# Decode attention finished beside the last gate pairs, and w_pc's stage fed one to two tiles ahead

## The chip, the cores and the metric

The kernel runs on one core of one Trainium2 chip. The metric is the device time of one execution in microseconds (us). The kernel before took 1598.49 us (median of three runs, 1595.0 to 1600.42). A difference within 0.3% (about 5 us) counts here as no change.

Engines are named as in the profile: PE (TensorE matmul), PEld (its weight loads), DVE (VectorE), ACT (ScalarE), POOL (GpSimd), SP (SyncE). SP and POOL issue nearly all DMAs, each in its own order.

## The reference, cut to what matters

```
h = RMSNorm_pre(x)
[q,k,v,ga | cb,cc,ch,gc | ma,mc] = h @ w_in
a = StickBreakingAttn(q,k,v) * silu(ga)       # 8 heads of 128; prompt: 528 tokens, causal
c = cb * conv3_causal(cc * ch) * silu(gc)
m = sigmoid(ma + b) * (a @ w_pa) + sigmoid(mc + b) * (c @ w_pc)
x = x + RMSNorm_post(m @ w_out)
# attention: A[t,s] = sigmoid(z_ts) * prod_{s<j<t} (1 - sigmoid(z_tj)), in log space
# decode: 8 sequences of 4 new tokens, each with 512 cached keys and values in 4 pages of 128
```

Prompt (512 tokens and 16 meta tokens) and decode (32 tokens) go through the same projections together: 560 columns, D_MODEL = 2048. All arithmetic is fp32: operands of the large products are split into a high and a low part and three matmuls are made of each product. Every weight block therefore passes through ACT (`whi`, L240) and DVE (`wlo`, L241) before TensorE may use it.

## The kernel before, in words

Order of the stages: norm and first queries; heads 0 to 3 attended at once (`head_now`); keys and values of heads 4 to 7 projected and put away in DRAM (`head_later`: `k_scr`, `vn_scr`, `qt_scr`); 36 gate pairs; the stage of `w_pc`; the stage of `w_pa`; the output projection.

**Gate pairs.** Each pair makes two 128-column blocks of `h @ w_in` with seven products of 24 matmuls (`seven`, L944). After each pair `dec_group()` (L875) is called, which takes some steps of the decode attention out of the generator `decode_steps()`. Steps 1 to 24 of it belong to the head stages. Then, in order: 40 steps of logits, each one page of keys (`kpage`) against four queries, 16 dot products on DVE (L754); the softmax in two steps and the exponentials in a third (L476, L800 to L815); eight steps of value products: each loads eight pages of values (`vpage`, L730, 9 buffers, issued by POOL) and multiplies them on TensorE (L829: 16 matmuls of four column groups, and in every second step 8 more with the new tokens' values), and every second step copies the sum out (`ob`, L849), transposes it (L852) and multiplies it into `sg_s` (L857). Softmax activations are pinned behind what stands before them on ACT, the value matmuls behind what stands before them on TensorE.

The counter `n` in `dec_group` sets at which pair the steps are emitted. Before: two per pair for n = 2 to 4, one for n = 5 to 20, then 2 and 1 in turn up to n = 32; softmax and exponentials at n = 34 to 36; then the first eight value pages are loaded; the value products come in the next stage.

The order on each engine is not the program's order. A scheduler of the library makes it when the kernel is built: among the instructions that its timing model holds ready it takes the first in program order, and a tile waits for a free buffer of its pool. [...]

**The stage of w_pc** (L1113 to L1155) makes 16 tiles `c @ w_pc` (48 matmuls each, L256, moving operand `c_hl`), multiplies each by its gate `gt` (loaded from `gate_scr`, L1150; L1153) and stores it again (L1154). Between the tiles heads 4 to 7 are attended (`HERE`: head 4 before tile 0, then before tiles 3, 6 and 9): scores (L608), softplus on ACT (L467 to L470) and DVE (L473 to L476), mask (L622), suffix products (L677), exponential (L681), output (L687). `gated` (L1124) multiplies an output by its gate rows and splits it into `a_hl` for the next stage. It is also called for heads 0 to 3, whose outputs lie in `a_scr`. In the kernel before

- the loads of `gt` (L1150), of the gate rows `sg` (L1129) and of `a_scr` (L1146) stand just ahead of their use, and share four buffers (pool `g3`, tag `gt`);
- the splits of a head's keys, values and queries (`khi`, `vhi`, `qhi`, L494 and L495) go into single buffers, just ahead of its scores;
- `dec_step(1)` before each tile takes one step of the value products.

Of the kernel before, what the change touches and what calls it, by code (L numbers as in the profile page):

```python
# [9 lines left out]
F32 = mybir.dt.float32  # L10
# [7 lines left out]
P = 128  # L18
D = 2048
KD = D // P  # L20
# [5 lines left out]
T = TP + TS  # L26
# [6 lines left out]
TQ = T - NMETA  # L33
HQ = TQ // 2
HU = HQ + 2
PQ = SEQ
# [6 lines left out]
H = 8  # L43
# [8 lines left out]
NOW = 4  # L52
# [8 lines left out]
def hybrid_step_kernel(  # L61
# [6 lines left out]
    nc = tc.nc  # L68
# [19 lines left out]
    def mm_ps():  # L88
        return ps.tile([P, 512], F32, tag="mm", name="mm", bufs=3)
# [4 lines left out]
    def o_ps():  # L94
        return ps.tile([P, 512], F32, tag="o", name="o", bufs=1)
# [148 lines left out]
    def weights(srcs):  # L244

        return [w_split(w_load(s)) for s in srcs]
# [210 lines left out]
    sg_scr = dram.tile([H, P, TQ], F32, name="sg_scr")  # L457
    a_scr = dram.tile([NOW, P, PQ], F32, name="a_scr")
# [4 lines left out]
    gate_scr = dram.tile([KD, P, 2, TQ], F32, name="gate_scr")  # L463
# [20 lines left out]
    d3ctx, hlctx, hctx, nctx = (ExitStack() for _ in range(4))  # L484
    hl = []
# [6 lines left out]
    def split_evac(hi, lo, raw_hi, raw_lo, scale=None):  # L492
        if scale is None:
            act.copy(hi, raw_hi)  # L494
# [53 lines left out]
    def k_split(pl, kr):  # L548
        khi = pl.tile([P, T], F32R, name="khi")
        klo = pl.tile([P, T], F32R, name="klo")  # L550
        split_evac(khi, klo, kr, kr)
        return khi, klo

    def v_split(pl, vn):
        vhi = pl.tile([P, 5, P], F32R, name="vhi", bufs=1)
        vlo = pl.tile([P, 5, P], F32R, name="vlo", bufs=1)
        split_evac(vhi[:, 0:4, :], vlo[:, 0:4, :], vn[:, 0:4, :], vn[:, 0:4, :])
        split_evac(vhi[0:16, 4, :], vlo[0:16, 4, :], vn[0:16, 4, :], vn[0:16, 4, :])
        return vhi, vlo
# [30 lines left out]
            return None  # L590
        return v_split(pl, vn)

    def attend(pl, h, khi, klo, vhi, vlo, qr, pl_a=None, after=None):

        qhi = pl.tile([P, T], F32R, name="qhi")
        qlo = pl.tile([P, T], F32R, name="qlo")
        split_evac(qhi[:, NMETA:TP], qlo[:, NMETA:TP], qr, qr)

        b = bsb[:, h:h + 1]
        gt = {}  # L600
# [33 lines left out]
        for g in GROUPS:  # L634
# [29 lines left out]
        ot = o_ps()  # L664
# [26 lines left out]
    def head_now(h):  # L691

        qr = hp.tile([P, TQ], F32, name="qr", bufs=2)[:, 0:PQ]
        nc.sync.dma_start(qr, qt_scr[h][:, 0:PQ])
        khi, klo = k_split(np_, k_proj(h))
        dec_step(1 if h else 0, "part")
        vhi, vlo = v_proj(h, np_)
        dec_step(1, "part")
        q_proj(NOW + h)
        dec_step(2, "part")  # L700
        ot = attend(np_, h, khi, klo, vhi, vlo, qr)
# [8 lines left out]
        v_proj(h)  # L710
        dec_step(2, "part")

    def head_loads(h):
        kr = hl[0].tile([P, T], F32, name="kr")
        nc.sync.dma_start(kr, k_scr[h])
        qr = hl[0].tile([P, PQ], F32, name="qr")
        nc.sync.dma_start(qr, qt_scr[h][:, 0:PQ])
        vn = hl[0].tile([P, 5, P], F32, name="vn")
# [154 lines left out]
    def dec_group():  # L873

        n = n_group[0] = n_group[0] + 1  # L875
        if n <= 32:
            dec_step((0, 2, 2, 2)[n - 1] if n <= 4 else 1 if n <= 20 else 1 + n % 2, "logits")
        else:
            dec_step(1)

    np_ = nctx.enter_context(tc.tile_pool(name="now", bufs=2))
    tc.keep_in_program_order(act.preload_act_table_set(LNEXP))
# [124 lines left out]
    def by_query(m, half):  # L1007
        return slice(half * HQ, (half + 1) * HQ)
# [61 lines left out]
    def q_tile(name):  # L1070
        return gp.tile([P, 2, HU], F32, tag="cv", name=name, bufs=3).rearrange("p a b -> p (a b)")[:, 0:TQ]
# [15 lines left out]
    for j in range(0, KD, 2):  # L1087
        for w, c in ((0, COL_MA), (1, COL_MC)):
            gs = [q_tile("g") for _ in range(2)]
            for m, half, b in pair(c + j * P, HQ):  # L1090
                act.activation(gs[m][:, by_query(m, half)], b, AF.Sigmoid, bias=gate_bias(j + m, w))
            if j + 2 * w == KD:
                tc.keep_in_program_order(act.preload_act_table_set(LNEXP))
            for m in range(2):
                gate_out(j + m, w, gs[m])
            dec_group()
            if j + w == 14:

                after = hl[0].tile([P, P], F32, name="after")
                dve.tensor_scalar_add(after, neg_u.bitcast(F32), 1.0)  # L1100
                loaded = head_loads(NOW)
    dec_step(64, "values")
    assert "values" in dec_at and "end" not in dec_at
    gctx.close()
    tctx.close()

# [1 line left out]
    QH = ((0, HQ), (HQ, TQ))  # L1108
    g3ctx, cctx, mctx = (ExitStack() for _ in range(3))
    g3 = g3ctx.enter_context(tc.tile_pool(name="g3", bufs=4))  # L1110
    c_hl = tok.tile([P, KD, TQ], F32R, tag="A", name="c_hl")
    a_hl = tok.tile([P, KD, TQ], F32R, tag="B", name="a_hl")
    cp = cctx.enter_context(tc.tile_pool(name="later", bufs=1))  # L1113
    cp2 = cctx.enter_context(tc.tile_pool(name="later2", bufs=1))

    for k in range(0, 8, 2):
        cr = g3.tile([P, 2, TQ], F32, tag="gt", name="cr")
# [4 lines left out]
    def gated(h, x, sg):  # L1122

        dve.tensor_mul(sg, x, sg)  # L1124
        split_evac(a_hl[:, h, 0:PQ], a_hl[:, 8 + h, 0:PQ], sg, sg)

    def sg_load(h):
        sg = g3.tile([P, 2, TQ], F32, tag="gt", name="sg")
        nc.sync.dma_start(sg[:, 0, 0:PQ], sg_scr[h][:, 0:PQ])  # L1129
        return sg  # L1130

    def head_here(h):
        kr, vn, qr = loaded if h == NOW else head_loads(h)
        ot = attend(cp, h, *k_split(cp, kr), *v_split(cp, vn), qr, cp2, after)
        gated(h, ot, sg_load(h)[:, 0, 0:PQ])


    HERE = {0: 4, 3: 5, 6: 6, 9: 7}
    for j in range(KD):
        if j in HERE:  # L1140
            head_here(HERE[j])
        dec_step(1)
        if j in HERE:
            k = j // 3
            x = sg_load(k)
            nc.sync.dma_start(x[:, 1, 0:PQ], a_scr[k])  # L1146
            gated(k, x[:, 1, 0:PQ], x[:, 0, 0:PQ])
        cs = slice(j * P, (j + 1) * P)
        gt = g3.tile([P, 2, TQ], F32, tag="gt", name="gt")[:, 1, :]
        nc.sync.dma_start(gt, gate_scr[j][:, 1, :])  # L1150
        oc = gemm(weights([w_pc[0][:, cs]]), lambda k: (c_hl[:, k, :], c_hl[:, 8 + k, :]), QH)
        for ob, s in qparts(oc):
            dve.tensor_mul(gt[:, s], ob, gt[:, s])  # L1153
        pool.dma_start(gate_scr[j][:, 1, :], gt)  # L1154
    dec_step(64)  # L1155
    split_evac(a_hl[:, 0:8, PQ:TQ], a_hl[:, 8:16, PQ:TQ], sg_s, sg_s)
    d3ctx.close()
    hlctx.close()
    dctx.close()
    cctx.close()  # L1160
# [7 lines left out]
    for k in range(8):  # L1168
        ms = []
        for j in (k, k + 8):  # L1170
            gt = g3.tile([P, 2, TQ], F32, tag="gt", name="gt")
# [7 lines left out]
        y, x = (ms[0][:, 1, slice(*s)] for s in QH)  # L1179
# [31 lines left out]
    with tc.tile_pool(name="outp", bufs=1) as op:  # L1211
# [107 lines left out]
        j = KD - 2  # L1319
# [117 lines left out]
```

## Time and profile before

| | us |
|---|---|
| median of three runs | 1598.49 |
| the profiled execution | 1598.94 |
| its span in the profile | 1597.3 |
| gate pairs, from 369 to 1139 of the span | 770 |
| stage of w_pc, from 1139.4 to 1307.8 | 168.4 |
| stage of w_pa, to 1405 | 97 |

Times inside the span count from its start. "Busy" is the time in which at least one instruction of the engine ran; in brackets stands the number of instructions. A row of waits reads: who waited, for whom, us in total, times, the longest. PEclk is the granted share of TensorE's clock.

### The profile page before, as it was taken

The page shows a single profiled execution, that of the slowest core. Times are in us where ns is not written, and L with a number is a line of the kernel's source. Part 1 is how long each engine was busy: PE and PEld are TensorE (multiplying, and loading weights), DVE is VectorE, ACT ScalarE, POOL GpSimd, SP SyncE. Part 2 cuts the span into 40 slices and gives each one's busy share as a digit, 9 for nine tenths or more (in the row PEclk, how much of TensorE's full clock was granted, in tenths as well). Part 3 has the DMA queues.
Part 4 walks back from the last instruction along what each step waited for, and adds up shares of the span by engine and source line. Part 5 has one row for each costly group of instructions (what it writes and reads, how often), then busy time and mean ns, then how long its engine had stood idle before and what let it go on. Part 6 is the DMA issues. An engine that isn't in the chain of part 4 may idle for free.

```text
span 1597.3 us, 32319 instructions
## 1 busy us (share of the span) xinstructions
PE 1567.6 (98%) x12172; PEld 1533.7 (96%) x12172; DVE 1268.8 (79%) x3574; ACT 752.7 (47%) x1339; POOL 234.6 (15%) x428
## 2 busy tenths in 40 slices
PE   9999999999999999999999999999899999999997
PEld 8999999999999999999999999999897789999997
DVE  6328999956799999999999996667666657877776
ACT  6335555435444444444454444446645543355562
POOL 1033333222111011010011100001203320000000
PEclk9999999999999999999999999999999999999999
DMA  8246556344555445355356554433868875433345
GB/s 247 81 137 180 169 164 187 110 127 138 167 162 146 139 140 150 117 152 159 107 180 187 161 155 130 125 121 115 279 186 265 253 240 179 152 101 99 100 137 187
DMA packets 300674, 252.77 MB, mean 158 GB/s; under 512 B 11521, under 2 KB 268613, under 8 KB 299701
## 3 DMA queue, kind: packets, MB, share of 16 engines
q1 hardware_dynamic: 272021, 160.45, 34.7%
q0 software_dynamic: 28368, 89.98, 17.0%
q8 instruction: 95, 1.56, 0.4%
q14 instruction: 62, 0.51, 0.1%
q10 hardware_dynamic: 128, 0.27, 0.1%
HBM read 217.95 MB, written 32.71 MB: 157 GB/s over the span
## 4 chain that ended last, share of the span: by engine, by line
PE 89%; DMA 4%; issue 2%; DVE 2%; ACT 1%; POOL 0%; DVEq 0%; POOLq 0%; SPq 0%; ACTq 0%
PE mm L944 32%; PE mm L256 24%; PE o L944 23%; DMA vpage<-in_cache_v 2%; PE mm L321 2%; PE z L321 1%; PE z L677 1%; PE o L687 1%; DMA raw<-in_w_in 1%; PE z L608 1%; PE z L1378 1%; DMA sg<-a_scr 1%; DMA gt<-gate_scr 1%; DVE wlo L241 1%; PE tp L829 0%
## 5 line engine op out<-in xcount | busy, mean ns | idle before, releaser
L240 ACT CAST whi<-raw 128x1024 fp32r<-128x1024 f32 x247 | 259.4, 1051 | 356.0 <-PE mm L944 122.3
L241 DVE TENSOR_TENSOR wlo<-raw,whi 128x1024 fp32r<-128x1024 f32 x247 | 301.2, 1221 | 82.9 <-ACT whi L240 81.5
L944 PE MATMUL mm<-h_hi,whi 128*128 128x272 f32 (+1 forms) x1152 | 332.6, 289 | 0.0
L944 PE MATMUL mm<-h_lo,whi 128*128 128x272 f32 (+1 forms) x1152 | 332.4, 289 | 0.0
L944 PE MATMUL mm<-h_hi,wlo 128*128 128x272 f32 (+1 forms) x1152 | 332.3, 290 | 0.0
L944 PE MATMUL o<-t_hi,whi 128*128 128x272 f32 (+1 forms) x864 | 250.0, 289 | 1.0 <-DVE c L970 1.0
L944 PE MATMUL o<-t_lo,whi 128*128 128x272 f32 (+1 forms) x864 | 250.2, 290 | 0.0
L944 PE MATMUL o<-t_hi,wlo 128*128 128x272 f32 (+1 forms) x864 | 249.8, 289 | 0.0
L754 DVE CUSTOM_DVE_ANT_0 junk<-kpage,qb 128x128 f32<-128x128 f32 x1024 | 245.1, 285 | 3.7 <-DMA qb<-q_scr 3.3
L944 PEld LDWEIGHTS mm<-h_hi,whi 128*128 128x128 f32 x1152 | 217.4, 189 | 0.0
L944 PEld LDWEIGHTS mm<-h_hi,wlo 128*128 128x128 f32 x1152 | 216.9, 189 | 0.1
L944 PEld LDWEIGHTS mm<-h_lo,whi 128*128 128x128 f32 x1152 | 216.8, 188 | 0.1
L241 DVE TENSOR_TENSOR wlo<-s,whi 128x1024 fp32r<-128x1024 f32 x126 | 154.0, 1222 | 63.9 <-ACT whi L240 62.5
L240 ACT CAST whi<-s 128x1024 fp32r<-128x1024 f32 x126 | 132.0, 1048 | 152.9 <-PE mm L944 52.8
L256 PE MATMUL mm<-h_lo,whi 128*128 128x280 f32 (+1 forms) x640 | 187.7, 293 | 0.0
L256 PE MATMUL mm<-h_hi,wlo 128*128 128x280 f32 (+1 forms) x640 | 187.1, 293 | 0.0
L256 PE MATMUL mm<-h_hi,whi 128*128 128x280 f32 (+1 forms) x640 | 186.7, 292 | 0.0
L944 PEld LDWEIGHTS o<-t_hi,whi 128*128 128x128 f32 x864 | 162.9, 189 | 1.5 <-DVE c L970 1.5
L944 PEld LDWEIGHTS o<-t_lo,whi 128*128 128x128 f32 x864 | 163.4, 189 | 0.5 <-issue 0.4
L944 PEld LDWEIGHTS o<-t_hi,wlo 128*128 128x128 f32 x864 | 163.1, 189 | 0.1
L256 PEld LDWEIGHTS mm<-h_lo,whi 128*128 128x128 f32 x640 | 120.4, 188 | 0.8
L256 PEld LDWEIGHTS mm<-h_hi,whi 128*128 128x128 f32 x640 | 120.5, 188 | 0.5
(390 smaller groups left out, 3181.1 us busy)
## 6 DMA issues: line engine op xcount, KB each, us to landing
raw<-in_w_in SPq DMA_DIRECT2D x192, 512.0 KB, 4.3
kpage<-in_cache_k POOLq DMA_DIRECT2D x64, 256.0 KB, 3.5
qb<-q_scr POOLq DMA_DIRECT2D x32, 512.0 KB, 5.7
vpage<-in_cache_v POOLq DMA_DIRECT2D x64, 256.0 KB, 5.8
raw<-in_w_out SPq DMA_DIRECT2D x32, 512.0 KB, 4.1
gate_scr<-g POOLq DMA_DIRECT2D x32, 272.0 KB, 4.6
gt<-gate_scr POOLq DMA_DIRECT2D x16, 544.0 KB, 3.9
raw<-in_w_pc SPq DMA_DIRECT2D x16, 512.0 KB, 4.4
```

The costliest lines, as they stand in the source:

```text
L240: act.copy(hi, x)
L241: dve.tensor_sub(lo, x, hi.bitcast(F32))
L256: pe.matmul(o, lhsT=w, rhs=r[:, t0:t1], start=(k == 0 and n == 0), stop=(k == nk - 1 and n == 2))
L321: pin(pe.matmul(o, lhsT=l, rhs=r[:, k, t0:t1], start=(start and m == 0), stop=(stop and m == 2), skip_group_check=True))
L608: pe.matmul(zt[:m, c0:c0 + n], lhsT=l[:, s0:s0 + m], rhs=r[:, ts:ts + n], start=(c0 == 0 and i == 0), stop=(i == 2), skip_group_check=True)
L677: pe.matmul(o, lhsT=l, rhs=x, start=False, stop=(i == len(ops) - 1), skip_group_check=True)
L687: pe.matmul(ot[:, ts - NMETA:ts - NMETA + n], lhsT=l[:m, st, :], rhs=x[:m, c0:c0 + n], start=False, stop=(g == GROUPS[-1] and i == 2), ski ...
L754: dve.tensor_tensor_reduce(out=junk, in0=kt[:, h * P:(h + 1) * P], in1=qt[:, t, h * P:(h + 1) * P], scale=1.0, scalar=0.0, op0=ALU.mult, o ...
L944: pe.matmul(o, lhsT=l[:, k, :], rhs=r, start=(start and k == 0 and m == 0), stop=(stop and k == 7 and m == 2), skip_group_check=True)
L1378: pin(pe.matmul(o, lhsT=(m1, m2)[h][:, k + 8 * (q == 1), ts], rhs=two[h][q == 2][:, :, k, :], start=(n == 0), stop=(n == 47)))
```

## The change

Decode: all 40 logits steps are emitted by n = 25, both softmax steps at n = 26, the exponentials at 27, first value loads and products at 28, then one value step per pair up to n = 35. Nothing of decode is left for w_pc's stage, and the pool of the value pages (`d3ctx`) is closed ahead of it.

w_pc's stage: the splits of a head go into one of two pools in turn (`split0`, `split1`), its inputs into one of two (`headin`, `headin2`); head 4 is split at the end of the gate pairs. Gate rows and outputs have a pool of their own with two buffers each (`gated`). `gt` is loaded one tile ahead and is now alone in its four buffers. Heads stand before tiles 0, 2, 5 and 8; the next head is loaded and split one tile after a head, and the outputs of heads 0 to 3 are gated two tiles after it. No transfer and no arithmetic is added or dropped.

```diff
-    def attend(pl, h, khi, klo, vhi, vlo, qr, pl_a=None, after=None):
-
+    def q_split(pl, qr):
         qhi = pl.tile([P, T], F32R, name="qhi")
         qlo = pl.tile([P, T], F32R, name="qlo")
         split_evac(qhi[:, NMETA:TP], qlo[:, NMETA:TP], qr, qr)
+        return qhi, qlo
+
+    def attend(pl, h, khi, klo, vhi, vlo, qhi, qlo, pl_a=None, after=None):
...
     def dec_group():

         n = n_group[0] = n_group[0] + 1
-        if n <= 32:
-            dec_step((0, 2, 2, 2)[n - 1] if n <= 4 else 1 if n <= 20 else 1 + n % 2, "logits")
+        if n <= 25:
+            dec_step((0, 2, 2, 2)[n - 1] if n <= 4 else 1 if n <= 20 else 4, "logits")
         else:
-            dec_step(1)
+            dec_step(2 if n in (26, 28) else 1)
...
-                loaded = head_loads(NOW)
-    dec_step(64, "values")
-    assert "values" in dec_at and "end" not in dec_at
+                loaded = head_loads(NOW, hl[0])
+    dec_step(64)
+    d3ctx.close()
+    hs0 = hlctx.enter_context(tc.tile_pool(name="split0", bufs=1, side="right"))
+
+    def head_split(pl, x):
+        kr, vn, qr = x
+        return *k_split(pl, kr), *v_split(pl, vn), *q_split(pl, qr)
+
+    parts = head_split(hs0, loaded)
     gctx.close()
     tctx.close()
...
+    ga = cctx.enter_context(tc.tile_pool(name="gated", bufs=2))
+    hs_ = hs0, cctx.enter_context(tc.tile_pool(name="split1", bufs=1))
+    hin = hl[0], cctx.enter_context(tc.tile_pool(name="headin2", bufs=1))
...
-    HERE = {0: 4, 3: 5, 6: 6, 9: 7}
+    HERE = {0: 4, 2: 5, 5: 6, 8: 7}
+    gts, sgs = {}, {}
+    gts[0] = gt_load(0)
+    sgs[NOW] = gate_load(NOW)
     for j in range(KD):
         if j in HERE:
-            head_here(HERE[j])
-        dec_step(1)
-        if j in HERE:
-            k = j // 3
-            x = sg_load(k)
-            nc.sync.dma_start(x[:, 1, 0:PQ], a_scr[k])
-            gated(k, x[:, 1, 0:PQ], x[:, 0, 0:PQ])
-        cs = slice(j * P, (j + 1) * P)
-        gt = g3.tile([P, 2, TQ], F32, tag="gt", name="gt")[:, 1, :]
-        nc.sync.dma_start(gt, gate_scr[j][:, 1, :])
-        oc = gemm(weights([w_pc[0][:, cs]]), lambda k: (c_hl[:, k, :], c_hl[:, 8 + k, :]), QH)
+            h = HERE[j]
+            ot = attend(cp, h, *parts, cp2, after)
+            gated(h, ot, sgs.pop(h))
+            sgs[h - NOW] = gate_load(h - NOW), out_load(h - NOW)
+        gt = gts.pop(j)
+        oc = gemm(weights([w_pc[0][:, j * P:(j + 1) * P]]), lambda k: (c_hl[:, k, :], c_hl[:, 8 + k, :]), QH)
         for ob, s in qparts(oc):
             dve.tensor_mul(gt[:, s], ob, gt[:, s])
         pool.dma_start(gate_scr[j][:, 1, :], gt)
-    dec_step(64)
+        if j + 1 < KD:
+            gts[j + 1] = gt_load(j + 1)
+        if j - 1 in HERE:
+            if h + 1 < H:
+                parts = head_split(hs_[(h + 1) % 2], head_loads(h + 1, hin[(h + 1) % 2]))
+                sgs[h + 1] = gate_load(h + 1)
+        if j - 2 in HERE:
+            k = HERE[j - 2] - NOW
+            sg, at = sgs.pop(k)
+            gated(k, at, sg)
     split_evac(a_hl[:, 0:8, PQ:TQ], a_hl[:, 8:16, PQ:TQ], sg_s, sg_s)
-    d3ctx.close()
```

More of the change, by code (lines that the diff above doesn't have):

```diff
@@ L700, in head_now @@
         dec_step(2, "part")
-        ot = attend(np_, h, khi, klo, vhi, vlo, qr)
+        ot = attend(np_, h, khi, klo, vhi, vlo, *q_split(np_, qr))
         dec_step(2, "part")
@@ L711, in head_later, with head_loads @@
         dec_step(2, "part")
-    def head_loads(h):
-        kr = hl[0].tile([P, T], F32, name="kr")
+    def head_loads(h, pl):
+        kr = pl.tile([P, T], F32, name="kr")
         nc.sync.dma_start(kr, k_scr[h])
-        qr = hl[0].tile([P, PQ], F32, name="qr")
+        qr = pl.tile([P, PQ], F32, name="qr")
         nc.sync.dma_start(qr, qt_scr[h][:, 0:PQ])
-        vn = hl[0].tile([P, 5, P], F32, name="vn")
+        vn = pl.tile([P, 5, P], F32, name="vn")
         nc.sync.dma_start(vn[:, 0:4, :], vn_scr[h][0:512].rearrange("(a p) d -> p a d", p=P))
@@ L1125, in gated, with gate_load, out_load, gt_load @@
         split_evac(a_hl[:, h, 0:PQ], a_hl[:, 8 + h, 0:PQ], sg, sg)
-    def sg_load(h):
-        sg = g3.tile([P, 2, TQ], F32, tag="gt", name="sg")
-        nc.sync.dma_start(sg[:, 0, 0:PQ], sg_scr[h][:, 0:PQ])
-        return sg
[L1132 to L1135, printed above, removed]
-    HERE = {0: 4, 3: 5, 6: 6, 9: 7}
+    def gate_load(h):
+        sg = ga.tile([P, PQ], F32, name="sg")
+        nc.sync.dma_start(sg, sg_scr[h][:, 0:PQ])
+        return sg
+    def out_load(h):
+        at = ga.tile([P, PQ], F32, name="at")
+        nc.sync.dma_start(at, a_scr[h])
+        return at
+    def gt_load(j):
+        gt = g3.tile([P, 2, TQ], F32, tag="gt", name="gt")[:, 1, :]
+        nc.sync.dma_start(gt, gate_scr[j][:, 1, :])
+        return gt
+    HERE = {0: 4, 2: 5, 5: 6, 8: 7}
+    gts, sgs = {}, {}
+    gts[0] = gt_load(0)
+    sgs[NOW] = gate_load(NOW)
     for j in range(KD):
         if j in HERE:
-            head_here(HERE[j])
-        dec_step(1)
-        if j in HERE:
-            k = j // 3
-            x = sg_load(k)
-            nc.sync.dma_start(x[:, 1, 0:PQ], a_scr[k])
-            gated(k, x[:, 1, 0:PQ], x[:, 0, 0:PQ])
-        cs = slice(j * P, (j + 1) * P)
-        gt = g3.tile([P, 2, TQ], F32, tag="gt", name="gt")[:, 1, :]
-        nc.sync.dma_start(gt, gate_scr[j][:, 1, :])
-        oc = gemm(weights([w_pc[0][:, cs]]), lambda k: (c_hl[:, k, :], c_hl[:, 8 + k, :]), QH)
+            h = HERE[j]
[4 more added lines that the diff above has]
+        oc = gemm(weights([w_pc[0][:, j * P:(j + 1) * P]]), lambda k: (c_hl[:, k, :], c_hl[:, 8 + k, :]), QH)
         for ob, s in qparts(oc):
```

## The prediction

> **What bounds the kernel now.** I read the engines' shares first, then the windows by stage, then the waits of the one stage in which TensorE is not full.
>
> ```profile
> PE 1567.6 (98%) x12172; PEld 1533.7 (96%) x12172; DVE 1268.8 (79%) x3574; ACT 752.7 (47%) x1339; POOL 234.6 (15%) x428
> ```
>
> ```profile
> core 0: us, PE busy (x) PEld busy (x) DVE busy (x) ACT busy (x) POOL busy (x), PEclk, DMA share, GB/s
> 390.00:1128.00 738.00, 736.96 (x5831) 735.54 (x5830) 653.50 (x1872) 341.54 (x499) 69.85 (x121) 1.00 0.49 145
> 1128.00:1308.00 180.00, 167.32 (x1222) 146.15 (x1221) 113.56 (x245) 94.27 (x159) 47.72 (x86) 0.96 0.80 254
> 1308.00:1405.00 97.00, 97.00 (x773) 97.00 (x772) 76.11 (x160) 35.74 (x61) 7.95 (x15) 1.00 0.51 155
> ...
> 1139.40:1307.80 168.40, 155.72 (x1135) 134.75 (x1135) 106.81 (x233) 86.93 (x150) 44.87 (x81) 0.96 0.78 249
> ```
>
> TensorE bounds the gate pairs and w_pa's stage outright. w_pc's stage, the last row, is the exception: 12.7 us of 168.4 idle, the clock at 0.96, DMA at 0.78. The waits of that stage:
>
> ```profile
> PE mm L256 <- DVE gt L1153: 10.1, 3, 5.8
> PE tp L829 <- DMA vpage<-in_cache_v: 1.4, 2, 0.7
> PE z L677 <- ACT l L494: 1.2, 1, 1.2
> ...
> DVE sg L1124 <- DMA sg<-a_scr: 12.1, 2, 8.2
> DVE gt L1153 <- DMA gt<-gate_scr: 9.1, 4, 4.0
> ...
> DVE gt L1153 <- PE tp L829: 4.3, 1, 4.3
> ...
> ACT vhi L494 <- PE o L687: 11.4, 3, 5.8
> ACT khi L494 <- PE z L608: 9.1, 2, 5.2
> ```
>
> TensorE's three rows make up its whole idle time: 10.1 + 1.4 + 1.2 = 12.7. The large one is second-hand. TensorE waits for PSUM that the gate multiplication (L1153) has not emptied, and DVE has not got there because it stands in order before a multiplication whose `a_scr` or `gt` rows have not landed.
>
> ```profile
> 1148.60:1154.30 5.70, 0.00 (x0) 0.00 (x0) 1.15 (x3) 1.38 (x2) 0.00 (x0) 0.94 1.06 374
> 1154.30:1160.50 6.20, 6.16 (x27) 6.16 (x28) 4.77 (x9) 0.73 (x2) 0.56 (x1) 0.50 0.71 205
> ...
> 1177.90:1179.90 2.00, 0.01 (x1) 0.00 (x0) 2.00 (x5) 0.00 (x0) 0.00 (x0) 1.00 0.21 48
> 1179.90:1184.40 4.50, 4.44 (x23) 4.44 (x24) 3.05 (x11) 1.16 (x2) 0.54 (x1) 0.62 0.72 219
> ...
> 1209.10:1211.40 2.30, 0.03 (x1) 0.00 (x0) 0.48 (x2) 0.37 (x1) 0.00 (x0) 1.00 1.02 395
> 1211.40:1215.10 3.70, 3.68 (x17) 3.69 (x18) 2.65 (x7) 1.42 (x3) 0.54 (x1) 0.54 0.99 373
> ```
>
> Read in pairs: after each of the three stalls (PE busy 0) the granted clock falls to 0.50, 0.62 and 0.54. That costs another 6.20 x 0.50 + 4.50 x 0.38 + 3.70 x 0.46 = 6.5 us. So the three stalls are worth 10.1 + 6.5 = 16.6 us.
>
> **The change part by part.**
>
> Earlier loads of `gt`, `sg` and `a_scr`. They are the same DMAs, issued one or two tiles ahead (a tile's 48 matmuls take 6.0 us at the 97.00 / 773 each of w_pa's row), from buffers that gate rows and `gt` no longer share. The chain of waits has the two worst of them:
>
> ```profile
> 1130.94 7.17 DMA raw<-in_w_pc
> 1141.71 11.32 DMA sg<-a_scr
> ...
> 1205.01 9.56 DMA gt<-gate_scr
> ```
>
> Those 11.3 and 9.6 us were taken at a DMA share of 0.8 to 1.06, with value pages in flight, which also leave. Two tiles cover the first; one tile covers most of the second. The third stall, DVE behind a tile held up by a value product (4.3), loses its cause too. I take all 16.6 us off. Bounds: 10.1 if the clock falls anyway, 19.2 if all 12.7 of idle time went.
>
> [...] The trace shows the fall after 2.0 and 2.3 us as well, so I keep the measured 6.5.
>
> The SP queue is given no further transfer, but loads now wait there for a free buffer ahead of weight loads. Weights are five buffers deep at one block per 6 us tile, so an SP wait up to the 11 us above is hidden.
>
> Value products moved.
>
> ```profile
> vpage<-in_cache_v POOLq DMA_DIRECT2D x64, 256.0 KB, 5.8
> ...
> 1139.40:1307.80 168.40, 19.35 (x160) 4.03 (x160) 0.96 0.78 249
> 1139.40:1307.80 168.40, 2.36 (x16) 1.92 (x16) 0.96 0.78 249
> ```
>
> The first row gives the loads, the other two the stage's L829 and L852 alone: 19.35 + 2.36 = 21.7 us of TensorE. They leave w_pc's stage, but the pairs have no room on TensorE, as these rows of four, one and one pairs show:
>
> ```profile
> 966.10:1050.60 84.50, 84.50 (x674) 84.50 (x673) 56.68 (x53) 39.66 (x56) 4.32 (x8) 1.00 0.42 127
> ...
> 1092.90:1116.50 23.60, 23.60 (x181) 22.83 (x180) 19.47 (x25) 16.37 (x24) 3.26 (x4) 1.00 0.40 121
> 1116.50:1139.50 23.00, 23.00 (x180) 22.79 (x179) 15.18 (x22) 16.33 (x23) 3.50 (x7) 1.00 0.77 229
> ```
>
> So the move is worth -21.7 + 21.7 = 0 in itself; whoever books the emptier stage as gain counts it twice. The copies, the `sg_s` products and 64 load issues on POOL lie beside TensorE: in the first row DVE has 28 of 84.5 us free, ACT 45, POOL 80.
>
> What it may cost is waiting. [...] Eight product steps cost 1.4 us so far, at a DMA share of 0.78. Beside the pairs I expect 0.42 plus the pages' 64 x 256 KB = 16.8 MB over eight pairs of 21.1 + 2.7 us (an estimate: 88 GB/s on top of 127, by the ratio of the first row 0.71). The conditions are much the same, but the cover is thinner, since nothing else holds TensorE up. I take 2.8, twice the row, +1.4. Bounds: -1.4, and +28.8 from landing times (rival C).
>
> Softmax moved. The last two pairs take 23.6 and 23.0 us where the others take 21.1. These 4.4 us go with the softmax to an earlier pair: 0. Bounds: -4.4 if nothing of it is repeated, +4.4 if it is paid twice.
>
> Logits in 25 pairs.
>
> ```profile
> L754 DVE CUSTOM_DVE_ANT_0 junk<-kpage,qb x1024: 260/283/724, 125.5 to 946.2; 128x128 f32<-128x128 f32 x171
> ...
> 881.50:946.50 65.00, 22.91 (x97) 1.00 0.50 152
> ```
>
> Pair 25 begins at 881.5 and has 21 us. 97 dot products then still lie ahead, and they lasted until 946. Forced through by the end of pair 25 they would need 22.9 us of DVE beside the pair's own 56.68 / 4 = 14.2: 37.1 in 21.1, 16 us too much. But emission is no deadline:
>
> ```profile
> 369.00:455.00 86.00, 13.19 (x56) 3.33 (x6) 1.00 0.53 162
> ...
> 451.92 0.28 DVE L754 CUSTOM_DVE_ANT_0 junk<-kpage,qb 128x128 f32<-128x128 f32 x1
> ...
> 452.13 0.29 DVE L754 CUSTOM_DVE_ANT_0 junk<-kpage,qb 128x128 f32<-128x128 f32 x1
> ...
> 452.43 0.43 DVE L975 TENSOR_TENSOR c<-mm,s 128x272 f32<-128x272 f32 x1
> 452.78 0.28 DVE L754 CUSTOM_DVE_ANT_0 junk<-kpage,qb 128x128 f32<-128x128 f32 x1
> ```
>
> The first row counts 56 dot products on DVE by 455, the end of pair 4, when six steps, 96 of them, had been emitted; so 40 were overdue. Still, the rows at 452 show a gate operation (L975) taken in after two of them: with two `junk` buffers the third is not ready at once. I expect logits to end near 946 as before, softmax right after, and values to have seven pairs: 0. Bounds: 0 and +16.
>
> Heads. Split a tile or more ahead into other buffers, the splits no longer stand on ACT waiting for the last head's scores and outputs (9.1 and 11.4 us of ACT, with the next softplus behind them). No instruction is added. With the value products gone, less work fills TensorE while a head's chain runs on DVE and ACT. The row for that is the 1.2 us of L677 on `l`; I take it once per head, 4 x 1.2 = 4.8, +3.6. Bounds: -1.2, and rival B. Head 4's early splits (eight copies and subtractions, each smaller than a weight block's) fit in the last pair, where ACT has 6.7 and DVE 7.8 us free.
>
> Sum on the profiled execution, 1598.94 us (span 1597.3; 0.45 above the median): -16.6 + 0 + 1.4 + 0 + 0 + 3.6 = -11.6, so 1587.3; for a median **1586.9**.
>
> **The rivals.**
>
> A, the forecast: 1587, own range 1580 to 1593.
>
> B, the chain of the heads sets the stage.
>
> ```profile
> L608 PE MATMUL z<-qhi,khi x40: 170/288/481, 118.3 to 1272.8; 128*128 128x400 f32 x8, 128*128 128x272 f32 x8, 128*128 128x144 f32 x8, 128*128 128x512 f32 x8
> ...
> L687 PE MATMUL o<-hiA,vlo x4: 395/397/397, 1200.4 to 1306.1; 128*128 128x512 f32 x4
> ```
>
> The heads' last output matmuls run from 1200.4 to 1306.1: (1306.1 - 1200.4) / 3 = 35.2 us per head, one after another, and the first scores stand at 1160.2. In the new kernel the stage begins 21.7 us later, at 1161. With the same 146 us from first score to last output it would end at 1307, where it ends now: 1598, no change. For it: strict succession. Against it: of the 25.5 us of DVE waits above all but the first 8.2 lie inside heads, and 11.4 of ACT; without them a head takes 35.2 - 17.3 / 4 - 11.4 / 4 = 28 us. TensorE's own work there is 168.4 - 12.7 - 6.5 - 21.7 = 127.5 us, so B decides from about 31 us per head on.
>
> C, slower: value pages arrive late beside the pairs. Landing took
>
> ```profile
> DMA to landing us min/median/max: 3.3/5.8/9.4
> ...
> POOL gate_scr L934 <- ACT g L1091: 207.9, 27, 18.5
> ```
>
> and POOL, which issues them, stands up to 18.5 us before a gate's store; a page queued behind such a store is late. If each of eight steps misses by 9.4 - 5.8 = 3.6 us, 28.8 us are lost instead of 2.8: 1587 + 27 = 1614. It turns the gain around from 1.8 us per step (14.4 in all). Against it: the loads of such a step were issued among the same kind of stores, at the same DMA share, for 1.4 us in all. [...]
>
> D, the logits' deadline: by strict program order DVE holds up pairs 23 to 26 by up to the 16 us: 1587 + 16 = 1603, just within no change.
>
> **How the numbers follow.** A 0.58; B 0.20, of which 0.04 with heads near 32 us still ends below 1594; C 0.14; D 0.08, of which 0.02 slower. 0.3% of 1598 is 5 us, about what a measurement of this kernel can tell from no change, so faster means under 1593.7: 0.58 + 0.04 = 0.62; same 0.16 + 0.06 = 0.22; slower 0.14 + 0.02 = 0.16. The range takes in A, B and most of D: 1579 (all 19.2 us) to 1600; A alone 1580 to 1593.
>
> **What would show it.** Gate pairs still at 1.00 busy, those with values near 23.8 us, dot products ending near 946, page waits under 4 us. w_pc's stage near 132 us, with the waits on `a_scr` and `gate_scr` gone and its clock at 1.00. I am wrong if pairs show waits on `vpage` above 14 us (C), if pairs 23 to 27 stretch (D), or if the stage keeps about 146 us with TensorE idle for `l`, `e` or `hi` (B).

## The result, and the profile after

The changed kernel takes 1590.28 us (median of six runs, 1588.02 to 1592.07), the kernel before 1598.02 (six runs beside them, 1595.0 to 1601.25): ratio 0.9949, 95% interval 0.9933 to 0.9965. It is faster by 0.5%, where 1586.9 (0.7%) was forecast. The profiled execution took 1588.02, its span is 1586.4, 10.9 less than before.

Line numbers up to about L590 are as before, from about L600 to the end of the gate pairs they are 2 higher, and behind that by more: the gate products are L946, the value products L831, scores L610, suffix products L679, exponential L683, output L689, gated multiplication L1136, the `gt` multiplication L1168.

The engines' shares, then the windows by stage (columns as before), the last two cutting w_pc's stage at 1290:

```profile
PE 1563.9 (99%) x12172; PEld 1528.4 (96%) x12172; DVE 1268.2 (80%) x3574; ACT 761.2 (48%) x1345; POOL 236.8 (15%) x428
```

```profile
1160.00:1302.50 142.50, 139.35 (x1026) 132.97 (x1024) 105.92 (x221) 83.24 (x142) 11.88 (x22) 0.97 0.60 185
...
1160.00:1290.00 130.00, 130.00 (x996) 126.80 (x994) 99.60 (x206) 79.04 (x134) 11.88 (x22) 1.00 0.65 203
1290.00:1310.00 20.00, 16.13 (x71) 12.95 (x71) 11.29 (x27) 6.95 (x13) 0.00 (x0) 0.66 0.04 10
```

The DMA share of the stage is down from 0.78 to 0.60. For 130 us TensorE is now full at full clock; all that the stage loses lies behind 1290: 20.00 - 16.13 = 3.9 us of idle time and 16.13 x 0.34 = 5.5 us of half clock, 9.4 together. The waits, from 1139 to 1310:

```profile
ACT vhi L494 <- PE o L689: 10.7, 2, 5.6
...
DVE gt L1168 <- PE mm L256: 7.3, 10, 2.2
...
ACT e L467 <- PE z L610: 5.3, 1, 5.3
...
PE o L689 <- ACT hi L494: 1.7, 1, 1.7
PE mm L256 <- ACT a_hl L494: 1.4, 1, 1.4
...
DVE sg L1136 <- DMA at<-a_scr: 1.1, 1, 1.1
```

The rows of 10.1 (TensorE on `gt`), 12.1 (`a_scr`) and 9.1 (`gate_scr`) are gone or down to about 1. DVE now waits for TensorE at L1168, not the other way. ACT still waits 10.7 us for outputs of heads (11.4 before). What TensorE still waits for is the end of head 7, as a few steps from the chain of waits show (start, duration, what):

```profile
1287.65 0.60 DVE rA L476
...
1291.39 0.55 ACT l L494
...
1292.45 2.36 PE z L679 x10
...
1295.34 0.68 ACT eA L683
...
1296.49 5.30 PE o L689 x15
...
1302.55 0.63 ACT a_hl L494
```

One head hops between DVE, ACT and TensorE. Nothing else is left for TensorE then:

```profile
L256 PE MATMUL mm<-c_hl,whi x512: 283/288/373, 1162.3 to 1281.4; 128*128 128x272 f32 x171
L256 PE MATMUL mm<-a_hl,whi x174: 282/288/594, 1281.7 to 1329.8; 128*128 128x272 f32 x174
L689 PE MATMUL o<-hiA,vlo x4: 388/397/628, 1204.6 to 1301.2; 128*128 128x512 f32 x4
```

The last of w_pc's products starts at 1281.4 (before at 1307.8); w_pa's products on heads that are done follow up to about 1290; head 7's last output matmul starts at 1301.2 (before 1306.1).

The pairs with decode, by windows: 28 to 36 before, then after, then pair 28 after alone:

```profile
944.90:1139.50 194.60, 194.60 (x1534) 193.62 (x1533) 136.66 (x150) 102.11 (x145) 14.32 (x25) 1.00 0.47 143
```

```profile
941.30:1161.20 219.90, 218.17 (x1717) 200.60 (x1716) 140.98 (x170) 113.24 (x160) 47.93 (x86) 1.00 0.67 207
941.30:967.30 26.00, 24.27 (x181) 22.99 (x180) 22.51 (x40) 23.85 (x32) 4.41 (x5) 1.00 0.45 134
```

They take 25.3 us more. TensorE's part of that by line: the value products, their transposes, and the scores of head 4 (L610) in pair 36:

```profile
941.30:1161.20 219.90, 19.35 (x160) 3.95 (x160) 1.00 0.67 207
941.30:1161.20 219.90, 2.40 (x16) 1.90 (x16) 1.00 0.67 207
...
1138.40:1161.20 22.80, 1.52 (x9) 1.35 (x10) 1.00 0.82 257
```

Decode's are 21.75, head 4's 1.52. The other 2.0 are put down to the softmax: pair 28, which holds both of its steps, has 26.00 - 24.27 = 1.73 of idle time.

The ledger of the spans, in us: up to pair 28 the changed kernel is 3.6 ahead (944.9 against 941.3), and 3.3 of that stands already where the first gate pair begins (369.0 against 365.7), ahead of all that was changed; the pairs cost 25.3 more; from there to the end it is 425.2 against 457.8, 32.6 less. Without the head start of 3.6 the change is worth 7.3, which agrees with the medians' 7.7.

### The profile page after: what moved, and what is told of

The parts are those of the page before. It is cut to its first block, busy times and chain, and to the rows that moved or that the text cites. A ratio compares the mean times of both kernels' runs of the same rounds, so it can differ in the third digit from the quotient of the medians.

```text
span 1586.4 us, 32330 instructions
## 1 busy us (share of the span) xinstructions
PE 1563.9 (99%) x12172; PEld 1528.4 (96%) x12172; DVE 1268.2 (80%) x3574; ACT 761.2 (48%) x1345; POOL 236.8 (15%) x428
## 4 chain that ended last, share of the span: by engine, by line
PE 95%; DVE 2%; ACT 1%; issue 1%; DMA 1%; DVEq 0%; ACTq 0%; SPq 0%
PE mm L946 33%; PE mm L256 27%; PE o L946 24%; PE mm L321 2%; PE z L679 1%; PE o L689 1%; PE z L321 1%; PE tp L831 1%; PE z L610 1%; PE z L1401 1%; PE tp L505 0%; PE z L1255 0%; DMA raw<-in_w_in 0%; DVE wlo L241 0%; PE tp L158 0%
## 5 line engine op out<-in xcount | busy, mean ns | idle before, releaser
L946 PE MATMUL mm<-h_hi,whi 128*128 128x272 f32 (+1 forms) x1152 | 333.5, 290 | 0.7 <-ACT whi L240 0.7
L946 PE MATMUL mm<-h_hi,wlo 128*128 128x272 f32 (+1 forms) x1152 | 332.6, 290 | 0.0
L946 PE MATMUL mm<-h_lo,whi 128*128 128x272 f32 (+1 forms) x1152 | 332.5, 289 | 0.0
L946 PE MATMUL o<-t_hi,whi 128*128 128x272 f32 (+1 forms) x864 | 250.2, 290 | 1.5 <-DVE c L972 1.5
L946 PE MATMUL o<-t_lo,whi 128*128 128x272 f32 (+1 forms) x864 | 249.8, 289 | 0.0
L946 PE MATMUL o<-t_hi,wlo 128*128 128x272 f32 (+1 forms) x864 | 249.6, 289 | 0.0
L946 PEld LDWEIGHTS mm<-h_hi,whi 128*128 128x128 f32 x1152 | 217.3, 189 | 6.1 <-ACT whi L240 3.5
L946 PEld LDWEIGHTS mm<-h_lo,whi 128*128 128x128 f32 x1152 | 216.8, 188 | 0.9 <-issue 0.8
L946 PEld LDWEIGHTS mm<-h_hi,wlo 128*128 128x128 f32 x1152 | 216.9, 189 | 0.2
L946 PEld LDWEIGHTS o<-t_hi,whi 128*128 128x128 f32 x864 | 162.8, 188 | 2.2 <-DVE c L972 2.2
L946 PEld LDWEIGHTS o<-t_hi,wlo 128*128 128x128 f32 x864 | 163.1, 189 | 0.9 <-issue 0.8
L946 PEld LDWEIGHTS o<-t_lo,whi 128*128 128x128 f32 x864 | 163.4, 189 | 0.0
L256 PEld LDWEIGHTS mm<-h_hi,wlo 128*128 128x128 f32 x640 | 120.5, 188 | 0.5
```

The lines of the kernel that those rows point to most:

```text
L256: pe.matmul(o, lhsT=w, rhs=r[:, t0:t1], start=(k == 0 and n == 0), stop=(k == nk - 1 and n == 2))
L946: pe.matmul(o, lhsT=l[:, k, :], rhs=r, start=(start and k == 0 and m == 0), stop=(stop and k == 7 and m == 2), skip_group_check=True)
```

## The experiments

Each kernel was compared with the kernel before on the same chip, and ratios are to it. In the first four the question was what made the gain and what ate the rest. Theory then: the early loads cure the stalls, and the chain of heads sets the end. Rival: the value pages' traffic had made the loads late; or TensorE's own work sets the end.

**Decode alone.** The loads, splits and buffers of the kernel before, with decode moved:

```
     def dec_group():
...
-        if n <= 32:
-            dec_step((0, 2, 2, 2)[n - 1] if n <= 4 else 1 if n <= 20 else 1 + n % 2, "logits")
+        if n <= 25:
+            dec_step((0, 2, 2, 2)[n - 1] if n <= 4 else 1 if n <= 20 else 4, "logits")
         else:
-            dec_step(1)
+            dec_step(2 if n in (26, 28) else 1)
...
-        dec_step(1)
         if j in HERE:
```

> The decode part alone: logits, softmax and values beside the gate pairs as in the changed kernel, w_pc's stage with its loads, buffers and order of heads as before (1598.0 us; changed 1590.3). Theory (moving TensorE work between two stages gains nothing, the gain of the change is the earlier loads): the stage still has its stalls at L1153 and begins 21 us later; 1598, within 5 of before. Rival (value pages in w_pc's stage made the loads late, so taking them out cures the stalls by itself): waits of DVE on a_scr and gate_scr under 8 us, 1590 or less.

Measured: 1592.46 us, ratio 0.9966 (0.9952 to 0.9981).

```profile
DVE sg L1124 <- DMA sg<-a_scr: 7.8, 4, 3.0
...
DVE gt L1152 <- DMA gt<-gate_scr: 2.9, 4, 1.0
...
PE mm L256 <- DVE gt L1152: 0.8, 2, 0.5
```

With unchanged loads, DVE's 21.2 us of waiting on `a_scr` and `gate_scr` are half gone (10.7), and TensorE's 10.1 on `gt` are 0.8. The move of decode, which the prediction booked at nothing, cures the three stalls almost wholly: the value pages and products had been in the loads' way. Whether by the pages' traffic, by their place in the queues or by the products that DVE waited for (4.3 before) isn't told apart. The result lies between the two expectations: 0.5 us under the theory's 1593, 2.5 above the rival's 1590, and the waits are 2.7 above its 8. Its interval overlaps the changed kernel's, so what the early loads add on top isn't resolved here.

**Loads alone.** Decode as before; loads and splits as in the change, with one set of split and input buffers:

```
...
-    hs_ = hs0, cctx.enter_context(tc.tile_pool(name="split1", bufs=1))
-    hin = hl[0], cctx.enter_context(tc.tile_pool(name="headin2", bufs=1))
+    hs_ = [cctx.enter_context(tc.tile_pool(name="split0", bufs=1))] * 2
+    hin = hl * 2
```

> The loads alone: value products stay in w_pc's stage, one step per tile as before; gate rows, outputs of heads 0 to 3 and gt are loaded one to two tiles ahead, heads stand before tiles 0, 2, 5 and 8. For want of room the splits and head inputs keep single buffers. Theory: the stalls at L1153 go, and the chain of heads starts near 1140 instead of 1160, so that it ends near 1280 and TensorE's work (149 us with the values) sets the end: 1584 to 1588, better than the changed kernel. Rival (the move of decode carries the gain, loads are late through the value pages): 1595 to 1600.

Measured: 1606.63 us, ratio 1.0043 (1.0025 to 1.006), slower than before, which neither side expected.

```profile
1140.62 10.90 DMA at<-a_scr
```

```profile
PE mm L256 <- DVE gt L1168: 6.6, 1, 6.6
```

```profile
L256 PE MATMUL mm<-c_hl,whi x501: 282/288/595, 1138.8 to 1280.8; 128*128 128x272 f32 x167
```

```profile
1281.00:1315.00 34.00, 25.29 (x127) 12.66 (x126) 15.94 (x41) 13.19 (x25) 9.29 (x17) 0.70 0.54 178
```

These are a step of its chain of waits, a wait, the matmuls of w_pc and a window. Issued early, among value pages, an `a_scr` row still took 10.9 us, and TensorE still stood 6.6 behind it, of the 10.1 before. DVE's waits on `gate_scr` are gone, but those on the rows of `sg_scr` and `a_scr` add up to 18.2. The tiles then ran ahead of the heads: w_pc's products were used up by 1280.8, and for 34 us, with the heads still to finish, TensorE lost 8.7 us idle and 25.29 x 0.30 = 7.6 to the clock. The heads end at 1314.5, 36.0 us apart. Early loads let the tiles run early, and then nothing covers the heads. Whether two sets of split buffers would have helped here isn't tested.

**Less TensorE work in the stage.** In the last eight tiles of w_pc a third of the products is left out (128 of 768 matmuls, about 16 us of TensorE at the 6.0 us of a tile's 48):

```
...
+                for n, (w, r) in enumerate(((hi[:, k, :], rh), (w[:, k, :], rl))):
+                    pe.matmul(o, lhsT=w, rhs=r[:, t0:t1], start=(k == 0 and n == 0), stop=(k == 7 and n == 1))
...
-        oc = gemm(weights([w_pc[0][:, j * P:(j + 1) * P]]), lambda k: (c_hl[:, k, :], c_hl[:, 8 + k, :]), QH)
+        oc = (gemm if j < 8 else gemm_hi)(weights([w_pc[0][:, j * P:(j + 1) * P]]), lambda k: (c_hl[:, k, :], c_hl[:, 8 + k, :]), QH)
```

> The changed kernel with 128 of 768 matmuls of w_pc's tiles left out (the low weight part in tiles 8 to 15), 16 us of TensorE work less in the stage. Theory (the four heads, one after another, set the end of the stage; TensorE idles behind head 7): the last output matmul stays near 1301, time 1588 to 1591, more idle time of TensorE instead. Rival (TensorE's work sets the length of the stage): 1574, the last output near 1285.

Measured: 1583.5 us, ratio 0.9903 (0.9876 to 0.9931): 0.46% less than the changed kernel, 7.4 of the 16 us and between the two expectations.

```profile
1258.00:1308.00 50.00, 39.70 (x221) 33.99 (x220) 35.17 (x81) 25.05 (x44) 2.69 (x5) 0.80 0.29 86
1160.00:1258.00 98.00, 98.00 (x754) 95.81 (x753) 80.19 (x159) 64.08 (x107) 9.17 (x17) 1.00 0.75 234
```

TensorE is full up to 1258 and then loses 10.3 us idle and 39.70 x 0.20 = 7.9 to the clock, 18.2 against the 9.4 of the changed kernel. About half of what is taken from TensorE comes back as waiting for heads. The last output matmul starts at 1295.5, which neither side expected (1301 and 1285), and heads come (1295.5 - 1205.5) / 3 = 30.0 us apart, not 32.2: how fast a head goes also depends on TensorE's other work.

**A shorter chain.** In the heads of w_pc's stage the correction term of the softplus is left out (three of its four operations on DVE, some 18 us over four heads), TensorE's work unchanged:

```
-            softplus_sums(e, l, r, t)
+            if after is None:
+                softplus_sums(e, l, r, t)
+            else:
+                dve.tensor_add(r, r, l)
```

> The changed kernel with a piece of each head's chain left out in w_pc's stage: the correction term of the softplus, three DVE operations on each of three groups, 4.6 us of DVE per head and 18 us in all; TensorE's work is the same. Theory (chain of heads): the last output matmul comes 10 to 16 us earlier, TensorE's idle time at the end goes, 1577 to 1582. Rival (TensorE's work sets the length, DVE has room): 1588 to 1591.

Measured: 1579.68 us, ratio 0.9878 (0.9851 to 0.9905).

```profile
1160.00:1310.00 150.00, 150.00 (x1145) 145.88 (x1144) 102.83 (x211) 91.30 (x156) 12.47 (x23) 1.00 0.62 189
```

```profile
L691 PE MATMUL o<-hiA,vlo x4: 393/398/398, 1200.3 to 1289.4; 128*128 128x512 f32 x4
```

No TensorE instruction was taken away, and TensorE is full throughout. Heads are 29.7 us apart, (1289.4 - 1200.3) / 3, instead of (1301.2 - 1204.6) / 3 = 32.2, and the kernel is 0.71% faster than the changed one. So the stage's end hangs on the heads' chain as well as on TensorE's work. Which of its links can be loosened with the whole computation kept was the next question: the hand-over of PSUM from head to head, or DVE's queue.

**A fourth bank.** A head's scores fill three PSUM banks (`z`); the bank `t_ps` of decode stands empty in this stage now. Group B of heads 4 and 6 gets it:

```
-            zt = z_ps()[:, :GW[g]]
+            zt = (t_ps if after is not None and g == "B" and h % 2 == 0 else z_ps)()[:, :GW[g]]
```

> Full computation. In w_pc's stage the scores of group B of heads 4 and 6 go to the PSUM bank that the decode transposes used, which stands empty there; so the first scores of the next head need not wait for the bank of the last head. Theory, the chain of heads sets the end of the stage and its links are the work inside a head plus what is queued ahead of it: the bank alone lets only the scores (about 2 us of TensorE a head) run ahead, the exponentials still find their tiles in use, so 1586 to 1590. Rival, what binds a head to the one before it is the PSUM bank alone: two of three hand-overs are freed, the last outputs come 8 us or more earlier, 1580 to 1583.

Measured: 1580.95 us, ratio 0.9895 (0.9879 to 0.991), about 8.6 us less than the changed kernel. First the changed kernel around heads 4 and 5 (exponentials of head 4, scores of head 5, its softplus), then the same of the fourth bank with the last output matmuls, and its window of the stage:

```profile
L683 ACT ACTIVATE eA<-z,bsb x1: 678/678/678, 1197.6 to 1197.6; 128x512 f32<-128x512 f32 x1
L610 PE MATMUL z<-qhi,khi x5: 172/289/440, 1199.4 to 1204.8; 128*128 128x400 f32 x1, 128*128 128x272 f32 x1, 128*128 128x144 f32 x1, 128*128 128x512 f32 x1
L467 ACT ACTIVATE e<-z,bsb x2: 593/595/597, 1206.1 to 1210.7; 128x416 f32<-128x416 f32 x2
```

```profile
L610 PE MATMUL z<-qhi,khi x5: 172/282/437, 1182.6 to 1202.2; 128*128 128x400 f32 x1, 128*16 128x16 f32 x1, 128*128 128x272 f32 x1, 128*128 128x144 f32 x1
L467 ACT ACTIVATE e<-z,bsb x2: 597/607/617, 1200.7 to 1203.0; 128x416 f32<-128x416 f32 x2
...
L689 PE MATMUL o<-hiA,vlo x4: 395/397/401, 1205.8 to 1294.7; 128*128 128x512 f32 x4
```

```profile
1160.00:1302.00 142.00, 141.58 (x1072) 136.96 (x1071) 111.34 (x231) 87.26 (x149) 11.93 (x22) 1.00 0.61 188
```

In the changed kernel head 5's scores start at 1199.4, once head 4's exponentials (the last starts at 1197.6) have emptied its banks, though its keys were split from 1176.4 on. With the fourth bank the first group starts at 1182.6 and softplus at 1200.7 instead of 1206.1. The tail is filled: 142 us lose 0.4. This theory had it that the bank alone brings little; it fell, and the rival's range held, though the last output moved by 6.5 us (1301.2 to 1294.7) and not by 8.

The bank is not all that sets the pace. In decode alone, without it, the last output matmuls are

```profile
L687 PE MATMUL o<-hiA,vlo x4: 395/397/628, 1216.5 to 1305.9; 128*128 128x512 f32 x4
```

(1305.9 - 1216.5) / 3 = 29.8 us apart. The changed kernel has the first of them 11.9 us earlier and the last only 4.7: most of the head start that the early splits give is lost on the way.

**The bank and three buffers.** `bufs=2 if after is None else 3` for groups B and C, and `hin = hl * 2`.

> Full computation. The kernel with the fourth bank, and three buffers instead of two for the softplus tiles of groups B and C; to make room, the head inputs are loaded into one buffer instead of two. Theory, chain of heads: now scores and exponentials of the next head can run beside the tail of the last one, the last output matmul comes 5 to 10 us before the 1301 it stands at, 1580 to 1586. Rival, the links are the operations of one head, not the buffers between heads: no change against the changed kernel, 1588 to 1592.

Measured: 1579.87 us, ratio 0.989 (0.9874 to 0.9906): at the lower edge of the theory's range (1580 to 1586), but the step from 0.9895 can't be told from none. TensorE is full for the whole stage (busy 142.00 us of 142.00, from 1160), so a shorter chain has nothing left to give there.

**The term on POOL.** Two operations of each softplus correction, 11.8 us in all, moved from DVE:

```
...
-            softplus_sums(e, l, r, t)
+            softplus_sums(e, l, r, t, dve if after is None else pool)
```

> Full computation. In w_pc's heads the two operations that form the softplus correction term are made on POOL instead of DVE (11.8 us less of DVE over four heads; POOL does only 11.9 us of DMA issue in this stage). Theory, the chain: the two operations are links of it on whichever engine; no POOL operation of this size is in the trace (its selects take 0.3 to 0.9 us for 112 to 128 columns), so if a POOL link is two to three times as long as the DVE one, the chain gains 12 us of DVE and loses about as much: 1586 to 1594. Rival, it is the DVE queue as a whole that sets the stage, not the chain: 1580 to 1585.

Measured: 1596.74 us, ratio 0.9997 (0.9986 to 1.0007), slower than the changed kernel by 0.5%. POOL's two operations, and the same on DVE in the changed kernel:

```profile
L473 POOL TENSOR_SCALAR lo<-e 128x416 f32<-128x416 f32 x8 | 14.0, 1748 | 16.2 <-ACT e L468 12.7 <-issue 2.3 <-DVE r L476 1.2
L474 POOL TENSOR_TENSOR lo<-e,lo 128x416 f32<-128x416 f32 x8 | 9.2, 1148 | 0.3
```

```profile
L473 DVE TENSOR_SCALAR lo<-e 128x416 f32<-128x416 f32 x8 | 2.9, 367 | 0.0
L474 DVE TENSOR_TENSOR lo<-e,lo 128x416 f32<-128x416 f32 x8 | 4.6, 580 | 0.1
```

DVE has less to do, POOL had little else (11.88 us busy of 142.5 in the changed kernel), and still every link of 0.95 us became one of 2.90. That refutes the rival (DVE's queue as a whole). The theory expected gain and loss to balance (1586 to 1594) and was missed by about 3 us. The operation with two inputs took twice as long on POOL as on DVE (1148 to 580 ns), the one with a single input 4.8 times (1748 to 367).

**Weights on POOL.** The low halves of w_pc's 16 weight tiles, no links of the chain, taken out of DVE's queue:

```
-        dve.tensor_sub(lo, x, hi.bitcast(F32))
+        eng.tensor_sub(lo, x, hi.bitcast(F32))
...
-        oc = gemm(weights([w_pc[0][:, j * P:(j + 1) * P]]), lambda k: (c_hl[:, k, :], c_hl[:, 8 + k, :]), QH)
+        oc = gemm(weights([w_pc[0][:, j * P:(j + 1) * P]], pool), lambda k: (c_hl[:, k, :], c_hl[:, 8 + k, :]), QH)
```

> Full computation. The low halves of w_pc's weight tiles (16 subtractions, 1.22 us each of DVE, 19.5 us in the stage) are made on POOL. They are no links of the heads' chain, but stand in DVE's queue between its links. Theory, a head's chain is lengthened by what DVE has queued ahead of its links: 35 us per head fall to 31 or 32, the last output comes 8 to 12 us earlier, 1579 to 1585. Rival 1, only the links themselves count: 1588 to 1591. Rival 2, POOL is so slow with 128x1024 (over 6 us, the pace of a tile) that TensorE waits for the low halves: over 1595.

Measured: 1592.95 us, ratio 0.9963 (0.9951 to 0.9975). The theory's range was missed by 8 us, and the first rival's by 2.

```profile
L241 POOL TENSOR_TENSOR wlo<-raw,whi 128x1024 fp32r<-128x1024 f32 x16 | 40.6, 2538 | 37.9 <-ACT whi L240 37.6
```

```profile
1160.00:1290.00 130.00, 123.80 (x923) 119.15 (x922) 100.33 (x177) 79.96 (x135) 50.39 (x34) 0.99 0.62 190
```

DVE was relieved of 19.5 us and heads came no faster (1210.6 to 1310.3, 33.2 us apart). That DVE's queue ahead of the links lengthens a head, which I had believed since the first four runs, isn't borne out. The profiled execution took 1597.34 us, 4.4 more than the median, so the trace may be a little worse than the usual run. TensorE's 6.2 us of idle time in this window are mostly waits on links of the heads (2.1 on `e`, 1.9 on `hi`, 1.3 on `l`); why they come earlier than in the changed kernel stays open, since the instruction order changed as well.

**The bank with late loads.** Decode moved, loads of before, and the fourth bank (the edits of the first and the fifth experiment):

> Full computation; the decode part of the change with the loads of before (1592.5 alone), plus the fourth PSUM bank for group B of heads 4 and 6. Theory, the bank hand-over ties the heads together and is the larger link: 8 to 11 us less than 1592.5, 1581 to 1585, whatever the loads do. Rival, without the earlier loads and second buffers the next head's inputs are not there to use the bank: 1588 to 1593.

Measured: 1587.15 us, ratio 0.9925 (0.9903 to 0.9947), between the expectations. Against decode alone the bank brings some 0.4%; against the bank with early loads 0.3% are missing, though the intervals overlap slightly. Early loads seem to be worth more once a bank lets scores use them (0.3%, against 0.2% without it), but neither step is resolved.

**The softmax spread over two pairs.** Softmax steps at n = 26 and 27, exponentials at 28; alone, then with the bank and three buffers, then with the values moved one step forward (`n in (29, 30)`):

```
-            dec_step(2 if n in (26, 28) else 1)
+            dec_step(2 if n == 29 else 1)
```

> Full computation; the changed kernel with the two softmax steps in pairs 26 and 27 instead of 26 with two steps, the exponentials in 28 and the value steps up to pair 36 (one pair with two steps, 29). Pairs 28 to 36 take 219.9 us in the changed kernel and 194.6 before, 25.3 more, of which the value products account for about 21.7. Theory, the surplus of 3.6 and the 1.7 us of idle TensorE in pair 28 come from two softmax steps in one pair: pairs end 1 to 4 us earlier and all after them moves with it, 1586.5 to 1589.5. Rival, the surplus is the products' own pace, or the last value step now delays the first head's splits: 1589.5 to 1594.

> Full computation; fourth bank, three buffers and the softmax spread over two pairs. With the bank TensorE is busy for all of the stage (142.00 of 142), so anything won in the pairs must show in full. Theory of the softmax's surplus: 1 to 4 us less than the 1579.9 of the bank with three buffers, 1576 to 1579. Rival: 1579 to 1582.

> Full computation; fourth bank and three buffers, the softmax steps in pairs 26 and 27, and two value steps in each of pairs 29 and 30, so that the value products end by pair 35 as in the changed kernel. With the softmax spread and the last value step behind the pairs, the pairs ended 4.4 us earlier but the first head of w_pc's stage started 10.6 us later. Theory: it was that last step that spoiled the saving, and TensorE is the bound of the stage once the bank is there; then the pairs' 3 to 4 us come through: 1575 to 1578 (ratio about 0.987). Rival: the pairs' surplus only moves to other pairs, 1579 to 1582 (ratio 0.989 to 0.990).

Measured: 1588.67 us, ratio 0.9934 (0.9914 to 0.9955); 1582.24, ratio 0.9893 (0.9872 to 0.9915); 1578.64, ratio 0.9887 (0.9869 to 0.9905). The first lies in the theory's range, the second just above both of its ranges, the third between its two. None can be told from its kernel without the spread; ranges 3 us wide were finer than these runs resolve. Pairs 28 to 36 alone and in the last of the three:

```profile
942.90:1156.90 214.00, 213.36 (x1684) 198.45 (x1686) 138.59 (x160) 108.21 (x152) 49.09 (x86) 1.00 0.68 207
```

```profile
944.70:1162.40 217.70, 217.70 (x1717) 200.57 (x1716) 141.24 (x170) 110.74 (x158) 48.98 (x86) 1.00 0.68 209
```

Where the values end by pair 35 the gain is 2.2 us of 219.9, the idle 1.73 among it: there, as expected, but under what the timing resolves. Alone, the pairs are 5.9 shorter; about half of that is one value step (21.75 / 8 = 2.7) that falls behind them, ahead of the first head. The last of the three, at 0.9887, is as fast as any full computation here and faster than the changed kernel (0.9949); the bank gives nearly all of that step.

## Why the prediction was right, and where it was not

The time fell in the range, 3.4 us above the forecast, and the sum holds in part on the trace: 7.3 measured without the head start, 11.6 forecast.

- **The three stalls, -16.6**: gone in full (no wait on `gt`, clock 1.00 up to 1290). The cause was only half right. The prediction credited the earlier loads and mentioned the pages in passing. The runs show the reverse: decode alone leaves 0.8 of the 10.1 us on `gt`, loads alone (with single split buffers) leave 6.6 and make the kernel slower. That the term held is partly luck: the change did both things.
- **Value products, 0**: right as a sum, 21.75 us of TensorE in the pairs instead of the stage. As a step it was wrong: it booked nothing for what leaves the stage with the products, the pages' 16.8 MB and DVE's wait for the products, and decode alone has 0.34% of the 0.51%.
- **Waits on pages, +1.4**: TensorE waits for no page, -1.4. Rival C had no place (its sum should read 1613: 28.8 in place of 2.8 is 26 more).
- **Softmax, 0**: +2.0, what is left of the pairs' 25.3, within its bounds.
- **Logits, 0**: right. The dot products end at 942.6 and the pairs before 28 keep their pace; D had no place.

```profile
L756 DVE DVE_READ_ACCUMULATOR2_ANT z_all<- x1024: 70/80/93, 122.4 to 942.6; 128x1 f32 x171
```

- **Heads, +3.6**: the step that failed. 1.2 us of waiting per head, spread evenly, was the wrong shape: nothing is lost while tiles are left, and 9.4 us in one tail behind head 7, over half of it half clock. Against the 1.2 of before that is +8.2. With the two small terms: -16.6 - 1.4 + 2.0 + 8.2 = -7.8, against the 7.3 measured.

The shortfall is rival B's mechanism. B was to decide from 31 us per head on; heads came 32.2 apart, not the 28 that the prediction got by taking DVE's and ACT's waits off the 35.2. DVE's waits on loads went, but ACT's on outputs did not: 10.7 of the 11.4 are still there. With two pools the splits of head 6 wait for the outputs of head 4, those of head 7 for head 5's, and both stand on ACT ahead of the next softplus. Nor would their removal alone have helped much: ahead of head 7's softplus no split is left, and there ACT waits 5.3 for its scores, which had to wait for PSUM banks (they start at 1269.4, head 6's last exponentials at 1267.7). That hand-over was in no term. So the outcome is the forecast's cure plus B in a mild form; B was set apart as a rival, and its 32 us case is what came. Decode alone, at 29.8 without the bank, shows that the hand-over does not fix the distance by itself; what else does stays open.

The expectation of a stage of 132 us failed accordingly: it takes 142.5.

## What to carry to other kernels

When a transfer is late, ask what else is in flight before loading it earlier: moving 64 value pages out of the stage did what issuing the loads ahead, alone, did not (0.8 us of TensorE's waits on `gt` left, against 6.6). When independent work covers a serial chain, compare where each ends, not the sums: the cover that ran out at 1290 decided, and freeing TensorE of 16 us gained only 7.4. Before a chain is fed earlier, look for the buffer that hands over from one pass to the next; one idle PSUM bank brought as much again as the whole change (8.6 us and 7.7).

## What the runs showed of the hardware

The clock fell to half without a long idle stretch of TensorE. Two short windows with the windows behind them, of the changed kernel and of the one with weights on POOL:

```profile
1290.20:1293.60 3.40, 2.67 (x14) 1.64 (x13) 2.61 (x7) 1.15 (x3) 0.00 (x0) 1.00 0.01 3
1293.60:1307.30 13.70, 10.57 (x37) 8.48 (x37) 6.70 (x16) 5.12 (x9) 0.00 (x0) 0.50 0.00 1
```

```profile
1266.40:1269.80 3.40, 2.61 (x18) 2.05 (x18) 2.79 (x3) 0.98 (x2) 2.45 (x2) 1.00 0.40 116
1269.80:1273.20 3.40, 3.40 (x18) 3.40 (x17) 2.31 (x6) 2.57 (x5) 0.00 (x0) 0.50 0.71 218
```

In the short windows TensorE was busy for 2.67 and 2.61 us and idle for 0.73 and 0.79, and the clock stood at 0.50 behind both, for 13.7 us where work stayed thin. In the first the longest wait was 0.7 us, in the second 0.8. But busy time alone doesn't decide it; in pair 28 of the changed kernel a window with less (2.12 us) kept the clock at 1.00 behind it:

```profile
960.80:964.20 3.40, 2.12 (x14) 1.63 (x12) 2.04 (x3) 3.38 (x4) 0.65 (x1) 1.00 0.00 0
964.20:967.60 3.40, 3.21 (x25) 3.21 (x26) 3.40 (x7) 1.63 (x3) 0.00 (x0) 1.00 0.00 0
```

What sets the fall is not shown. In the changed kernel the tail of short dependent matmuls cost 5.5 us of clock on top of 3.9 us of idle time.

In the kernel before, DVE stood idle for 8.18 us, up to 1153.15, until `a_scr` rows landed (L1124). The low halves of head 4's keys and queries came behind that on DVE, at 1154.55 and 1156.00, though ACT had started their high halves at 1146.20 and 1147.47 and needed 0.6 us for each.
